# Long-convolution taps moved into the head stage, and output rows finished by ScalarE and accumulating transfers

## The chip, the cores and the metric

The kernel runs on one core of one Trainium2 chip. Its engines are TensorE (PE in the profile, with PEld for its weight loads), VectorE (DVE), ScalarE (ACT), GpSimd (POOL) and SyncE (SP, which issues most transfers). The metric is the device time of one execution in microseconds (us); a kernel's time is the median of its runs. SBUF is the on-chip memory that all engines read and write, PSUM the smaller one that TensorE writes its products into.

## The reference

One layer of a hybrid encoder on 512 rows of 2048 float32 values:

```python
h = rmsnorm(x, g_pre);  proj = h @ w_in
qkv, z_a, b, a, glu_in, z_b, gate_logits = split(proj)
# branch a: 16 heads of gated DeltaNet (conv of 4, chunks of 64, a triangular solve per chunk)
q, k, v = heads(silu(causal_conv(qkv, w_conv_qkv)))
o = gated_delta_chunked(l2norm(q), l2norm(k), v, g_log, beta)
y_a = (rmsnorm(o, g_dn_out) * silu(z_a)) @ w_br_a
# branch b: gated linear unit, causal depthwise convolution of 31 taps, layer norm over channels
u = causal_depthwise_conv(glu(glu_in), w_dw) + b_dw
y_b = (silu(layernorm(u, ln_g, ln_b)) * silu(z_b)) @ w_br_b
mixed = (gate_a * y_a + gate_b * y_b) @ w_out
x = x + rmsnorm(mixed, g_post)
e = p @ w_ple_proj
out = x + rmsnorm(sigmoid(x @ w_ple_gate) * e, g_ple)
```

## The kernel before

**Data.** Activations lie with channels on the 128 partitions and the 512 rows along the free axis in the first stages: a *channel tile* is 128 channels x 512 rows, and there are 16 of them for a width of 2048. At the end, rows lie on partitions: four *row tiles* of 128 rows, each in four column parts of 512. A float32 product is made of three matmuls, from a high and a low half of each operand (L183, L185 and L187 in `gemm_cm`). The halves of a weight piece are made on the fly by `prep`: ScalarE casts the high half (L126), and `low_part[0]` subtracts it from the raw weights to give the low half (L127). `low_part[0]` is VectorE, and GpSimd for a while in stage 2.

**What sets the order.** Matmul jobs stand in a list and run one after the other. After each 512-wide matmul, `tick()` counts down the generators that `spawn` has started; a generator whose count is zero runs to its next `yield n`, which means n more matmuls. So other engines' work is placed among the matmuls by counting them, and each engine executes in the order that results. `pin` keeps an instruction at its place in the program; the others may be reordered a little.

**Stages.** Loading and normalising x (to about 55 us); the z gates by a Strassen-like scheme (to 550); the heads (550 to 1487); *stage 2* (to 1960): the remaining gated pairs, the long convolution, branch a, layer norm; then branch b, the output projection and the end.

**Heads.** Eight pairs of heads, numbered 0 to 7 here. For each, six matmul tiles (k, q, v of two heads) and two tiles out of the deque `rest` are run, then `group(g)` is spawned. In `rest` stand the silu-gate tiles (`zb_tile`) and then the gated linear unit's tiles (`glu_b`, then `glu_a`). `group` goes: W on VectorE from a product in PSUM (L866, L867); four copies Ud on ScalarE, VectorE, GpSimd, VectorE (L881); a transpose UT (L887); the *triangular loop*, 31 steps of a multiplication (L898, both inputs in SBUF) and a reduction (L899) on VectorE, each depending on the last; a transpose Vd (L906); copies VP on ScalarE (L912) and transposes Tc on VectorE (L913); then TensorE's small products py (L919) and pz (L922), which need Tc, and pd (L934); then `head_scan` for both heads (psA L757, psB L763, psS L769, the output's transpose po L797). `scanning[0]` holds the number of the last pair whose scan has begun. VectorE also evacuates and convolves the q, k, v tiles there (L710) and makes the low weight halves (L127). In the same stage `presums` sums weight blocks in DRAM by 192 transfers from GpSimd's queue (L1070, L1075).

**Long convolution.** A finished gated tile u (L1041) goes into `waiting`. `convs` takes channel tiles from there, one at a time, and applies 30 taps on VectorE (L1011), `pace(s)` matmuls apart; in stage 2 `near` first copies u into PSUM (`up`), in the heads u is read from SBUF (`sg`). `side_convs` does two channel tiles in stage 2, each tap as a ScalarE product (L1032, `pr`) and a GpSimd addition (L1033). Finished tiles are added up for layer norm (`filtered`, L975 and L977); the sums over channels are matmuls (sum_ps L1195, the variance L1210, rstd_ps L1222).

**The end.** The gate product of the last step (L1635 to L1637) with its weight pieces from `split_piece` (ScalarE cast L1616, VectorE low half L1617) runs through a plan; after each quarter `step()` issues up to three of the queued `chores`. `gate_steps` weighs the embedding (sigmoid L1943, product L1944, square L1946, gain L1949); `final_steps(tt)` finishes a row tile: `inv_rms` (L1574, L1575 on VectorE, the power L1577 on GpSimd) and four times L1965 on VectorE (scale and add x1) with a store L1966. Row tiles 0 and 1 are `LOW`; tiles 2 and 3 come last, and the last tile's product is finished in two halves (L2038).

## Time and profile before

| | us |
|---|---|
| median of 3 runs (2391.45, 2393.43, 2393.59) | 2393.43 |
| the profiled execution, its own time | 2393.88 |
| span of the profiled execution, first to last instruction | 2391.8 |
| TensorE busy in the span | 2366.5 |
| VectorE busy in the span | 1909.5 |
| ScalarE busy in the span | 1230.6 |
| GpSimd busy in the span | 548.8 |
| VectorE busy in the heads (937 us) / in stage 2 (473 us) | 690.8 / 426.1 |
| GpSimd busy in the heads / in stage 2 | 213.5 / 263.5 |

The mean granted TensorE clock was 0.997 of full speed. The profile lists, per engine, line and operation, the busy time, the mean time of one in ns, and what ended the idle time before. A row of the timeline gives the start, the time until the last of the "xN" instructions ended, the engine, the line, what is written and read, and in brackets the idle time before and what released it.

### The profile page before, as it was taken

What the parts mean: (1) busy time and instruction counts of PE and PEld (TensorE: products, weight loads), DVE (VectorE), ACT (ScalarE), POOL (GpSimd) and SP (SyncE); (2) the same over time, 40 slices, a digit from 0 to 9 for tenths busy, and PEclk for the clock granted to TensorE, in tenths of its full rate; (3) what the DMA queues carried; (4) which work ended last, traced back from release to release, by engine and by line L of the source; (5) the groups of instructions that cost most, each with busy time, mean ns of one, the idle gap of its engine ahead of it and who ended that gap; (6) DMA issues with size and microseconds to landing.
All of it is one profiled execution on the core that took longest, in us unless ns stands there. A gap on an engine that the chain in (4) does not pass through costs nothing.

```text
span 2391.8 us, 33735 instructions
## 1 busy us (share of the span) xinstructions
PE 2366.5 (99%) x11774; PEld 1949.1 (81%) x11774; DVE 1909.5 (80%) x3517; ACT 1230.6 (51%) x2405; POOL 548.8 (23%) x591
## 2 busy tenths in 40 slices
PE   9999999999999999999999999999999999999997
PEld 7888888887888888888888887888888888888885
DVE  8877888786777786767777777999998897887877
ACT  6455455555644545454544544554423665665654
POOL 1001100011122122231321230798861000000000
PEclk9999999999999999999999999999999999999998
DMA  7577766665476768687874883443353577766565
GB/s 277 163 192 209 203 202 198 202 182 186 149 223 174 205 200 252 175 227 196 220 237 146 211 247 106 149 150 106 115 167 119 185 251 239 257 221 223 194 226 167
DMA packets 152186, 463.57 MB, mean 194 GB/s; under 512 B 17744, under 2 KB 26192, under 8 KB 150480
## 3 DMA queue, kind: packets, MB, share of 16 engines
q1 hardware_dynamic: 122608, 336.10, 41.9%
q0 software_dynamic: 27104, 121.13, 21.6%
q10 hardware_dynamic: 2304, 4.20, 0.6%
q8 instruction: 92, 1.51, 0.3%
q14 instruction: 78, 0.64, 0.1%
HBM read 426.22 MB, written 132.12 MB: 233 GB/s over the span
## 4 chain that ended last, share of the span: by engine, by line
PE 89%; DVE 4%; issue 2%; DMA 2%; ACT 2%; POOL 0%; SPq 0%; DVEq 0%; POOLq 0%; ACTq 0%
PE g L185 13%; PE g L187 13%; PE g L183 13%; PE zp L473 6%; PE zp L472 6%; PE zp L471 6%; PE f L1637 4%; PE f L1635 4%; PE f L1636 4%; PE yp L1466 2%; PE yp L1462 2%; PE yp L1464 2%; PE yp L1141 2%; PE yp L1143 2%; PE yp L1139 2%
## 5 line engine op out<-in xcount | busy, mean ns | idle before, releaser
L185 PE MATMUL g<-hl,w 128*128 128x512 f32 x1536 | 610.4, 397 | 0.0
L187 PE MATMUL g<-hh,w 128*128 128x512 f32 x1536 | 608.4, 396 | 0.0
L183 PE MATMUL g<-hh,w 128*128 128x512 f32 x1536 | 608.1, 396 | 0.0
L126 ACT CAST w<-raw 128x512 fp32r<-128x512 f32 x564 | 346.0, 617 | 415.6 <-PE g L187 240.7
L127 DVE TENSOR_TENSOR w<-raw,w 128x512 fp32r<-128x512 f32 x450 | 309.6, 695 | 86.4 <-ACT w L126 83.9
L185 PEld LDWEIGHTS g<-hl,w 128*128 128x128 f32 x1536 | 289.0, 188 | 55.4 <-issue 1.4
L183 PEld LDWEIGHTS g<-hh,w 128*128 128x128 f32 x1536 | 289.2, 188 | 54.1
L187 PEld LDWEIGHTS g<-hh,w 128*128 128x128 f32 x1536 | 289.1, 188 | 53.9 <-POOL w L127 0.3
L1011 DVE SCALAR_TENSOR_TENSOR uc<-up,vec,uc 128x497 f32<-128x497 f32 (+29 forms) x390 | 282.3, 733 | 13.2 <-ACT uc L990 1.9
L127 POOL TENSOR_TENSOR w<-raw,w 128x512 fp32r<-128x512 f32 x114 | 146.4, 1298 | 57.2 <-ACT w L126 55.1
L1635 PE MATMUL f<-wsp,oph 128*128 128x512 f32 x352 | 137.8, 391 | 0.0
L710 DVE SCALAR_TENSOR_TENSOR cv<-g,vec,cv 128x511 f32<-128x511 f32 x144 | 106.4, 739 | 39.2 <-ACT cv L708 38.9
L1636 PE MATMUL f<-wsp,opl 128*128 128x512 f32 x352 | 137.4, 390 | 0.0
L1637 PE MATMUL f<-wsp,oph 128*128 128x512 f32 x352 | 137.2, 390 | 0.0
L1617 DVE TENSOR_TENSOR wsp<-raw,wsp 128x1024 fp32r<-128x1024 f32 x81 | 98.5, 1221 | 31.0 <-ACT wsp L1616 25.5
L1616 ACT CAST wsp<-raw 128x1024 fp32r<-128x1024 f32 x81 | 83.8, 1048 | 63.1 <-PE f L1636 38.2
L1141 PE MATMUL yp<-w,oh 128*128 128x512 f32 x256 | 100.1, 391 | 0.0
L1143 PE MATMUL yp<-w,ol 128*128 128x512 f32 x256 | 99.5, 391 | 0.0
L1139 PE MATMUL yp<-w,oh 128*128 128x512 f32 x256 | 99.1, 389 | 0.0
L898 DVE TENSOR_TENSOR prod<-UT,VT 128x2 f32<-128x2 f32 (+30 forms) x248 | 87.2, 352 | 6.5
L1033 POOL TENSOR_TENSOR uc<-uc,pr 128x511 f32<-128x511 f32 (+29 forms) x60 | 75.7, 1262 | 8.3 <-ACT pr L1032 7.7
L1637 PEld LDWEIGHTS f<-wsp,oph 128*128 128x128 f32 x352 | 66.1, 188 | 13.9
(435 smaller groups left out, 4878.7 us busy)
## 6 DMA issues: line engine op xcount, KB each, us to landing
raw<-in_w_in SPq DMA_DIRECT2D x194, 512.0 KB, 3.7
wb_sums<-in_w_br_b POOLq DMA_DIRECT2D x48, 512.0 KB, 8.9
wo_sums<-in_w_out POOLq DMA_DIRECT2D x48, 512.0 KB, 8.9
wp_sums<-in_w_ple_gate POOLq DMA_DIRECT2D x48, 512.0 KB, 9.2
raw<-in_w_br_a SPq DMA_DIRECT2D x32, 512.0 KB, 3.3
raw<-wb_sums SPq DMA_DIRECT2D x32, 512.0 KB, 4.3
raw<-wp_sums SPq DMA_DIRECT2D x32, 512.0 KB, 3.7
raw<-in_w_ga SPq DMA_DIRECT2D x24, 512.0 KB, 5.1
```

The source lines that it names most:

```text
L126: nc.scalar.copy(hi, rq)
L127: low_part[0].tensor_tensor(lo, rq, hi.bitcast(F32), ALU.subtract)
L183: mm(ps, wh, rh, start=(k == 0), stop=False)
L185: mm(ps, wh, rl, start=False, stop=False)
L187: mm(ps, wl, rh, start=False, stop=(k == NK - 1))
L1011: pin(nc.vector.scalar_tensor_tensor(y[:, s:], u[:, 0:T - s], vv(w0 + TAPS - 1 - s), y[:, s:], ALU.mult, ALU.add))
L1139: mm(ps[tt], lh[:, b], wh, start=k == 0, stop=False)
L1141: mm(ps[tt], lh[:, b], wl, start=False, stop=False)
L1143: mm(ps[tt], ll[:, b], wh, start=False, stop=k == NK - 1)
L1635: mm(ps, lh, wh[:, c], start=kk == 0, stop=False)
L1636: mm(ps, ll, wh[:, c], start=False, stop=False)
L1637: mm(ps, lh, wl[:, c], start=False, stop=kk == 7)
```

## The change

Five things are edited.

1. `rest` holds the tiles of gated pairs 0 to 3 first, then the silu-gate tiles, then pair 4. The same 21 tiles run, seven of them after the last pair of heads.
2. `side_heads` is new, spawned with pair 1 of the heads: two channel tiles, each tap a ScalarE product (`pr`), 10 matmuls later a GpSimd addition, and 14 matmuls later the next one. `side_convs` with its two tiles in stage 2 stays.
3. `convs` is spawned with pair 3 and begins when pair 3's scan has begun, not pair 7's. While heads 3 to 6 are scanned, its taps are 18 matmuls apart. Two channel tiles are done in the heads; ten are left for VectorE's taps afterwards.
4. `with_x` stores x1 of row tiles 0 and 1 to `out` by eight transfers from GpSimd's queue, and the final steps of these tiles are a ScalarE scaling in place and a GpSimd transfer that accumulates into `out`. They are issued from a queue of their own, `scalings`, two per step.
5. The final steps of row tile 2 are woven between those of tile 3, after all matmuls.

TensorE executes the same instructions; psA, psB and psS of pair 3's scan stand up to six matmuls later, the last pair's po up to seven earlier, and the layer norm's sums 214 earlier.

```diff
--- before.py
+++ after.py
@@ -991,11 +991,11 @@
         return i, u, y
 
     def pace(s):
-        return (3 + s % 2 if taken_ps[0] else 4) if ups else CP
+        return (3 + s % 2 if taken_ps[0] else 4) if ups else CP if scanning[0] == NH // 2 - 1 else 18
 
     def convs():
         ready = last = None
-        while scanning[0] < NH // 2 - 1:
+        while scanning[0] < 3:
             yield 4
         while len(done) < NK:
             ready = ready or near()
@@ -1021,6 +1021,21 @@
                 taken_ps[0] = True
                 low_part[0] = nc.gpsimd
 
+    def side_heads():
+        for _ in range(SIDE):
+            while not waiting:
+                yield 4
+            i, u, y = near(False)
+            w0 = V_DW + i * TAPS
+            for s in range(1, TAPS):
+                pr = slots.tile([P, T], F32, tag="s", name="pr")
+                nc.scalar.activation(pr[:, s:], u[:, 0:T - s], AF.Copy, scale=vv(w0 + TAPS - 1 - s))
+                yield 10
+                pin(nc.gpsimd.tensor_tensor(y[:, s:], y[:, s:], pr[:, s:], ALU.add))
+                yield 14
+            nc.sync.dma_start(u_dram[i], y)
+            filtered(i, y)
+
     def side_convs():
         for _ in range(SIDE):
             while not waiting or not taken_ps[0]:
@@ -1079,7 +1094,8 @@
             for jp in range(2):
                 yield from f(jp, *args)
 
-    rest = deque([lambda i=i: zb_tile(i) for i in range(FILL, NK)] + [f for i in range(2) for f in (lambda i=i: glu_b(i), lambda i=i: glu_a(i))])
+    both = [f for i in range(5) for f in (lambda i=i: glu_b(i), lambda i=i: glu_a(i))]
+    rest = deque(both[:8] + [lambda i=i: zb_tile(i) for i in range(FILL, NK)] + both[8:])
     for g in range(NH // 2):
         pair = (2 * g, 2 * g + 1)
         for h in pair:
@@ -1089,6 +1105,10 @@
         jobs.append(lambda g=g: spawn(group(g), HP, "heads"))
         if g == 0:
             jobs.append(lambda: spawn(presums(), 16, "presum"))
+        if g == 1:
+            jobs.append(lambda: spawn(side_heads(), 8, "convs"))
+        if g == 3:
+            jobs.append(lambda: spawn(convs(), CP, "convs"))
         for _ in range(2):
             if rest:
                 rest.popleft()()
@@ -1096,9 +1116,8 @@
     mixed = [[None] * 4 for _ in range(NTT)]
     gate_b = [[None] * 4 for _ in range(NTT)]
 
-    jobs.append(lambda: spawn(convs(), CP, "convs"))
-    for i in range(2, 5):
-        glu_pair(i)
+    while rest:
+        rest.popleft()()
     run_jobs()
     finish("heads")
     heads_ctx.close()
@@ -1723,6 +1742,8 @@
         def with_x(j):
             for n, tt in enumerate(tts):
                 pin(nc.vector.scalar_tensor_tensor(x1[tt][j], x1[tt][j], rm[:, n:n + 1], xr.pop((tt, j)), ALU.mult, ALU.add))
+                if tt in LOW:
+                    nc.gpsimd.dma_start(rows(out, tt, j), x1[tt][j])
 
         def turn(k2, ps):
             for n in range(4):
@@ -1898,12 +1919,17 @@
 
     passed = [0]
 
+    scalings = deque()
+
     def step():
         next(xgen, None)
         passed[0] += 1
         for _ in range(2 if passed[0] < 20 else 3):
             if chores:
                 chores.popleft()()
+        for _ in range(2):
+            if scalings:
+                scalings.popleft()()
 
     pair = [-1]
 
@@ -1962,8 +1988,12 @@
 
         def one(j):
             e = e_t[tt, j]
+            if tt in LOW:
+                pin(nc.scalar.activation(e, e, AF.Copy, scale=rp))
+                pin(nc.gpsimd.dma_start(rows(out, tt, j), e, accum_op=ALU.add))
+                return
             pin(nc.vector.scalar_tensor_tensor(e, e, rp, x1[tt][j], ALU.mult, ALU.add))
-            nc.sync.dma_start(out[tt * P:(tt + 1) * P, j * T:(j + 1) * T], e)
+            nc.sync.dma_start(rows(out, tt, j), e)
         return [lambda j=j: one(j) for j in range(4)]
 
     v = {}
@@ -1999,7 +2029,7 @@
                 chores.append(chore_tt(d[t], ps[t], d[t], ALU.add))
             gated_out(LOW, 2 * jp + 1, d)
             if jp:
-                chores.append(lambda: chores.extendleft(reversed(final_steps(0) + final_steps(1))))
+                chores.append(lambda: scalings.extend(final_steps(0) + final_steps(1)))
         elif pr == "P7":
             u, s5 = v["P1", jp], v["Q5", jp]
             for t in range(2):
@@ -2020,28 +2050,28 @@
         for q in range(4):
             mms(ps[t], "Q4", last[q], q, t, x1_opnd)
             step()
-        while chores and t:
-            chores.popleft()()
         if t == 0:
-            late = deque([chore_tt(u[0], ps[0], u[0], ALU.add), *gate_steps(2, 2, u[0]), lambda: late.extendleft(reversed(final_steps(2)))])
-
-            def follow():
-                while late:
-                    late.popleft()()
-                    chores.append(follow)
-                    return
-            chores.append(follow)
-        else:
-            halves_ = [gate_steps(3, 2, u[1], h) for h in range(2)]
-            for h in range(2):
-                cs = slice(h * 256, h * 256 + 256)
-                pin(nc.vector.tensor_tensor(u[1][:, cs], ps[1][:, cs], u[1][:, cs], ALU.add))
-            for h in range(2):
-                halves_[h][0]()
-            for h in range(2):
-                halves_[h][1]()
-            for f in final_steps(3, 5):
-                f()
+            chores.append(chore_tt(u[0], ps[0], u[0], ALU.add))
+            chores.extend(gate_steps(2, 2, u[0]))
+    while chores:
+        chores.popleft()()
+    while scalings:
+        scalings.popleft()()
+    halves_ = [gate_steps(3, 2, u[1], h) for h in range(2)]
+    third = final_steps(2)
+    for h in range(2):
+        cs = slice(h * 256, h * 256 + 256)
+        pin(nc.vector.tensor_tensor(u[1][:, cs], ps[1][:, cs], u[1][:, cs], ALU.add))
+    third[0]()
+    for h in range(2):
+        halves_[h][0]()
+        third[1 + h]()
+    for h in range(2):
+        halves_[h][1]()
+    fourth = final_steps(3, 5)
+    third[3]()
+    for f in fourth:
+        f()
 
 
 def _cm_tiles(w, cols):
```

The first place is VectorE in pair 5's triangular loop. Before (`UT`, `VT` and `prod` are the loop's tiles, `w` and `raw` a weight piece):

```order
L898 TENSOR_TENSOR prod<-UT,VT 128x4
L899 TENSOR_REDUCE VT<-prod 128x1
L898 TENSOR_TENSOR prod<-UT,VT 128x10
L127 TENSOR_TENSOR w<-raw,w 128x512
L899 TENSOR_REDUCE VT<-prod 128x2
L898 TENSOR_TENSOR prod<-UT,VT 128x12
L899 TENSOR_REDUCE VT<-prod 128x2
L898 TENSOR_TENSOR prod<-UT,VT 128x14
```

In the changed kernel (`sg` is u, `uc` the channel tile's running sum):

```order
L898 TENSOR_TENSOR prod<-UT,VT 128x4
L899 TENSOR_REDUCE VT<-prod 128x1
L898 TENSOR_TENSOR prod<-UT,VT 128x10
L127 TENSOR_TENSOR w<-raw,w 128x512
L899 TENSOR_REDUCE VT<-prod 128x2
L1011 SCALAR_TENSOR_TENSOR uc<-sg,vec,uc 128x509
L898 TENSOR_TENSOR prod<-UT,VT 128x12
L899 TENSOR_REDUCE VT<-prod 128x2
L898 TENSOR_TENSOR prod<-UT,VT 128x14
L899 TENSOR_REDUCE VT<-prod 128x2
```

A tap of the long convolution (L1011) now stands between two steps of the loop, and so on at about every fourth step. The shapes of the loop's steps are the same.

The second place is GpSimd in pair 2 of the heads, in the changed kernel; before, only the transfers and the copies stood there (`wb_sums` and `wo_sums` are the weight sums in DRAM, `kq` a copy for the heads):

```order
L1085 DMA wb_sums<-in_w_br_b 128x1024
L1034 TENSOR_TENSOR uc<-uc,pr 128x488
L1085 DMA wb_sums<-in_w_br_b 128x1024 x2
L1034 TENSOR_TENSOR uc<-uc,pr 128x487
L1085 DMA wb_sums<-in_w_br_b 128x1024
L1034 TENSOR_TENSOR uc<-uc,pr 128x486
L1085 DMA wb_sums<-in_w_br_b 128x1024 x2
L1034 TENSOR_TENSOR uc<-uc,pr 128x485
L1085 DMA wo_sums<-in_w_out 16x8192
L1034 TENSOR_TENSOR uc<-uc,pr 128x484
```

The side taps' additions (L1034, `uc` plus `pr`) stand one by one between the transfers of `presums` (L1085 here, L1070 before).

The third place is VectorE at the end of the program. Before, from the last product of row tile 2 on:

```order
L1949 TENSOR_TENSOR e<-e,grow 128x512
L1574 TENSOR_REDUCE totp_21951<-ssp 128x1
L1575 TENSOR_SCALAR totp_21951<-totp_21951 128x1
L1965 SCALAR_TENSOR_TENSOR e<-e,rmsp_21954,snap 128x512
L1965 SCALAR_TENSOR_TENSOR ew<-ew,rmsp_21954,snap 128x512
L1965 SCALAR_TENSOR_TENSOR e<-e,rmsp_21954,u_20161 128x512
L1965 SCALAR_TENSOR_TENSOR e<-e,rmsp_21954,snap 128x512
L2038 TENSOR_TENSOR snap<-f,snap 128x256 x2
L1944 TENSOR_TENSOR e<-snap,e 128x256 x2
L1949 TENSOR_TENSOR e<-e,grow 128x256 x2
L1574 TENSOR_REDUCE totp_21986<-ssp 128x1
L1575 TENSOR_SCALAR totp_21986<-totp_21986 128x1
```

In the changed kernel L1965 is L1995, L1944 is L1970, L1949 is L1975 and L2038 is L2064:

```order
L1975 TENSOR_TENSOR e<-e,grow 128x512
L1593 TENSOR_REDUCE totp_22085<-ssp 128x1
L1594 TENSOR_SCALAR totp_22085<-totp_22085 128x1
L2064 TENSOR_TENSOR snap<-f,snap 128x256 x2
L1995 SCALAR_TENSOR_TENSOR e<-e,rmsp_22088,snap 128x512
L1970 TENSOR_TENSOR e<-snap,e 128x256
L1995 SCALAR_TENSOR_TENSOR ew<-ew,rmsp_22088,snap 128x512
L1970 TENSOR_TENSOR e<-snap,e 128x256
L1995 SCALAR_TENSOR_TENSOR e<-e,rmsp_22088,u_20275 128x512
L1975 TENSOR_TENSOR e<-e,grow 128x256 x2
L1593 TENSOR_REDUCE totp_22106<-ssp 128x1
L1594 TENSOR_SCALAR totp_22106<-totp_22106 128x1
```

Tile 2's four final steps stood ahead of tile 3's half additions and stand between tile 3's steps now. Eight L1965 of row tiles 0 and 1, which stood further ahead, are gone from VectorE.

## The prediction

> **What bounds the kernel now.** I read the page's busy shares first, then TensorE's waits, then the stretches in which another engine is nearly as full, and last the end.
>
> ```profile
> span 2391.8 us, 33735 instructions
> PE 2366.5 (99%) x11774; PEld 1949.1 (81%) x11774; DVE 1909.5 (80%) x3517; ACT 1230.6 (51%) x2405; POOL 548.8 (23%) x591
> PE po L797 <- DVE O L793: 1.6, 2, 0.8
> PE rstd_ps L1222 <- DVE dg L1217: 0.8, 1, 0.8
> PE f L1637 <- DVE wsp L1617: 0.7, 1, 0.7
> PE sum_ps L1195 <- POOL acc L977: 0.4, 1, 0.4
> ```
>
> TensorE is busy 99% of the span and its longest waits are under a microsecond (columns: total, times, longest). The change keeps every matmul. So it can win only these waits and what lies behind the last matmul; it loses whatever new wait TensorE gets. The losing side is much the longer one.
>
> Where is the cover thin? In the heads, each pair of heads has a stretch from W (L866) through the triangular loop (L898/L899) to the Tc transposes (L913), on which py (L919) waits. For pair 5, first VectorE and then TensorE:
>
> ```profile
> 1181.07 0.43 DVE L866 SCALAR_TENSOR_TENSOR W<-pg,E 128x256 f32<-128x256 f32 x1 [0.55 <-PE pg L862]
> 1221.59 1.38 DVE L913 STREAM_TRANSPOSE Tc<-VP 32x256 f32<-32x256 f32 x3
> 1225.37 0.69 PE L919 MATMUL py<-Tc,W 32*32 32x32 f32 x32
> 1198.48 0.69 DVE L127 TENSOR_TENSOR w<-raw,w 128x512 fp32r<-128x512 f32 x1 [0.84 <-ACT w L126]
> 1181.00:1223.00 42.00, 38.78 (x95) 1.00 0.67 206
> 1073.60:1181.00 107.40, 80.62 (x194) 1.00 0.73 201
> ```
>
> Tc ends at 1222.97 and py starts at 1225.37: slack 2.4 us. VectorE is busy 38.78 of 42.00 us there, with one removable gap, 0.84. So a stretch hides about 3.25 us of added VectorE time; beyond that py is late, and with it everything on TensorE. Over a whole pair (107.4 us) VectorE is busy 80.62, so work outside the stretch has room. The end is the second place:
>
> ```profile
> 2374.02 0.39 PE L1637 MATMUL f<-wsp,oph 128*128 128x512 f32 x1
> 2361.66 0.75 DVE L1965 SCALAR_TENSOR_TENSOR ew<-ew,rmsp,c 128x512 f32<-128x512 f32 x1 [0.60 <-POOL rmsp L1577]
> 2368.58 0.75 DVE L1965 SCALAR_TENSOR_TENSOR ew<-ew,rmsp,d 128x512 f32<-128x512 f32 x1
> 2369.24 1.28 DVE L1953 TENSOR_TENSOR snap<-f,snap 128x512 f32<-128x512 f32 x2
> 2381.65 0.75 DVE L2038 TENSOR_TENSOR snap<-f,snap 128x256 f32<-128x256 f32 x2
> 2385.30 0.75 DVE L1965 SCALAR_TENSOR_TENSOR e<-e,rmsp,snap 128x512 f32<-128x512 f32 x1 [0.66 <-POOL rmsp L1577]
> 2387.29 0.75 DVE L1965 SCALAR_TENSOR_TENSOR e<-e,rmsp,snap 128x512 f32<-128x512 f32 x1
> 2387.40 1.00 SPq L1966 DMA_DIRECT2D out_dram<-e  x2
> ```
>
> The last matmul ends at 2374.4; the tail of 17.4 us is VectorE's: it still works off row tiles 0 and 1 when the last products arrive, then tile 2, then tile 3.
>
> **The change, part by part.**
>
> *The end: -4.5 us.* Eight L1965 (four per tile 0 and 1) leave VectorE for ScalarE and accumulating transfers; from 2361.66 and 2362.33 they start 0.66 to 0.67 apart: 8 x 0.66 = 5.3 us of VectorE's work. Not all shows: the second weight piece in the row now waits for ScalarE's casts behind four scalings, so the L1953 pair starts about 2.9 us earlier (2366.3). Tile 3's half additions (L2038) no longer stand behind tile 2's four L1965; by walking the new order with the old durations they start near 2375.4 instead of 2381.65. In exchange those four are woven between tile 3's steps and cost +1.7 there, so the last group starts near 2380.6 instead of 2385.30. I take -4.5, with bounds -2.5 (weights' casts later still) and -5.5 (all 5.3 shows); it is 0 if one of the eight accumulating transfers lands last.
>
> *Layer norm: -1.0.* Ten channels instead of fourteen are left for VectorE after the heads, so the sums come 214 matmuls earlier in TensorE's order, and between the variance and rstd_ps there are 12 matmuls instead of 7. Five matmuls of 0.227 us (the L183 rows below) cover the 0.8 us wait. Bounds -1.2 and 0.
>
> ```profile
> 1224.15 0.39 PE L183 MATMUL g<-hh,w 128*128 128x512 f32 x1
> 1224.83 0.39 PE L183 MATMUL g<-hh,w 128*128 128x512 f32 x1
> ```
>
> Three matmuls in 0.68 us.
>
> *Taps of VectorE in pairs 4 to 6: +4.5.* convs() now starts its taps (L1011) with pair 3's scan, one in 18 matmuls. What does an instruction cost inside the loop?
>
> ```profile
> 1189.60 0.17 DVE L898 TENSOR_TENSOR prod<-UT,VT 128x4 f32<-128x4 f32 x1
> 1189.79 0.16 DVE L899 TENSOR_REDUCE VT<-prod 128x1 f32<-128x4 f32 x1
> 1189.99 0.18 DVE L898 TENSOR_TENSOR prod<-UT,VT 128x10 f32<-128x10 f32 x1
> 1190.08 0.69 DVE L127 TENSOR_TENSOR w<-raw,w 128x512 fp32r<-128x512 f32 x1
> 1190.68 0.16 DVE L899 TENSOR_REDUCE VT<-prod 128x2 f32<-128x10 f32 x1
> L1011 DVE SCALAR_TENSOR_TENSOR uc<-up,vec,uc 128x511 f32<-128x511 f32 (+5 forms) x297 | 217.4, 734 | 11.7 <-ACT uc L990 1.9
> ```
>
> From an L898 to its L899 it is 0.19 us without an L127 between and 0.69 with one: it costs 0.50, since it fills part of a dependent wait. A tap lasts 0.734 against 0.69, so I take 0.55 in the loop and 0.66 outside it. By the new order of VectorE, pair 4's stretch gets 9 taps (7 in the loop): 3.9 + 1.3 = 5.2; pair 5's 9 (8 in the loop) and one more L127: 5.5; pair 6's 7 and one L127, less one L1041: 3.7. Less 3.25 each: 1.95 + 2.25 + 0.45 = 4.65, taken as 4.5. Bounds: 0 (the transposes and copies hide more than I see) and 9.9 (0.66 everywhere, the 0.84 gap not filled).
>
> *Side taps on GpSimd in pairs 1 to 4: +11.2.* Each of the 60 puts an activation on ScalarE (51% busy, hidden) and a two-input addition on GpSimd. That would be free but for this, from the last part of the heads:
>
> ```profile
> L1011 DVE SCALAR_TENSOR_TENSOR uc<-sg,vec,uc x6: 718/726/1803, 1499.5 to 1504.2; 128x487 f32<-128x487 f32 x1, 128x486 f32<-128x486 f32 x1, 128x485 f32<-128x485 f32 x1, 128x484 f32<-128x484 f32 x1
> 1501.51 1.41 POOL L127 TENSOR_TENSOR w<-raw,w 128x512 fp32r<-128x512 f32 x1 [12.25 <-ACT w L126]
> 1504.23 1.29 POOL L127 TENSOR_TENSOR w<-raw,w 128x512 fp32r<-128x512 f32 x1 [1.31 <-ACT w L126]
> L1033 POOL TENSOR_TENSOR uc<-uc,pr x60: 1223/1262/1300, 1510.7 to 1745.6; 128x511 f32<-128x511 f32 x2, 128x510 f32<-128x510 f32 x2, 128x509 f32<-128x509 f32 x2, 128x508 f32<-128x508 f32 x2
> L898 DVE TENSOR_TENSOR prod<-UT,VT 128x2 f32<-128x2 f32 (+30 forms) x31 | 10.9, 352 | 0.8
> L127 DVE TENSOR_TENSOR w<-raw,w 128x512 fp32r<-128x512 f32 x13 | 8.9, 687 | 0.8 <-ACT w L126 0.8
> ```
>
> VectorE's taps that read both inputs from SBUF take 0.726 us (middle number), but up to 1.803 where GpSimd's additions run: up to 1.08 lost to one. The 297 taps with the input in PSUM keep their mean of 0.734 while GpSimd works on side taps. In the stretch L898 and L127 have both inputs in SBUF, 10.9 + 8.9 of 42 us, so an addition of 1.26 us almost always meets one; where a one-input instruction runs first, part is covered. I take 0.65 as the mean loss, an estimate; bounds 0.3 and 1.08. The stretch has 180 matmuls, one side tap in 24: 7.5, so 4.9 us. Pairs 1 to 3 also get one GLU product (0.5): 0.5 + 4.9 - 3.25 = 2.1 each, 6.3; in pair 4, where the taps have used the cover, all 4.9. Bounds of this part: +2.2 and +23.7.
>
> The Trainium skill, "SBUF — State Buffer", section "Who interferes with whom", says that a VectorE instruction with two SBUF inputs contends with a GpSimd instruction that reads SBUF, and that the loser is fully blocked for the whole instruction. The rows agree as to which taps suffer (1.803 against 0.734). By the full 1.26 us the stretch would lose an estimated 9.4 us, and this part would come to about 29.
>
> *Scans and weights outside the stretches: +1.* In pair 4 VectorE's 80.6 us become about 80.6 + 21 x 0.62 + 16 x 0.65 = 104 of 107.4, so weights and scans may be late now and then; 0 to 3. *Row stores of x1 by GpSimd, eight transfers near 2200: 0*, beside loads that have room; 0 to 1.5.
>
> **Sum.** -4.5 - 1.0 + 4.5 + 11.2 + 1 + 0 = +11.2. The profiled execution of 2393.9 us (span 2391.8 and 2.1 around it) becomes 2405.1, the span 2403.0. The median of the runs shown is 2393.43, 0.5 lower: **2404.6 us**.
>
> **Rivals.**
> 1. *Everything fits (the other side).* If the stretches hide all that is added, for instance because GpSimd's additions fall behind its own transfers into idle time and the taps fill waits, only the end and layer norm count: -5.5, 2387.9. It decides as long as py's slack is not used up, that is, while a stretch grows by no more than 3.25 us. For it: scans, copies and transposes leave gaps. Against it: nine taps alone make 5.2.
> 2. *No loss to GpSimd, but taps count.* Side taps are free: -5.5 + 4.5 + 1 = 0, 2393.4. Against it: the 1.803.
> 3. *Full blocking.* Each side tap costs 1.08, and VectorE, full in pair 4, delays scans by 2: -5.5 + 4.5 + 23.7 + 2 = +24.7, 2418.1. For it: both overlapped taps lost nearly this much; against it: L899 and L710 run alongside.
> 4. *The end is not won*, since GpSimd issues eight accumulating transfers in a row: +15.7, 2409.1.
>
> **Chances.** Forecast 0.42, own range 2396 to 2413; rival 1 0.16, rival 2 0.20, rival 3 0.14, rival 4 0.08. A measurement here can tell about 0.2%, 4.8 us, from no change. Faster by more: most of rival 1 and a little of rival 2, 0.16. Within: most of rival 2, the low end of the forecast, the rest of rival 1, 0.28. Slower: 0.56. Range 2388 to 2416: it leaves out half of rival 1 and of rival 3.
>
> **What would show it.** Right: waits of py on Tc in pairs 1 to 6, longest in pair 4 (about 6.9 us), none in pairs 0 and 7; L127 and L898 with longer means in pairs 1 to 4 than in 5 to 7; no wait at rstd_ps; the last group of L1965 starting about 6.2 us after the last matmul ends, not 10.9. Wrong: py without waits (rival 1), waits in pairs 4 to 6 alone (rival 2), ScalarE waiting for GpSimd to free a product's buffer and the casts queued behind it, or an accumulating transfer as the last to land.

## The result, and the profile after

The changed kernel takes 2450.06 us (2448.39 to 2452.86); the kernel before, run beside it, 2393.51 us. The ratio is 1.0238, with a 95% interval of 1.0225 to 1.0251: 56.6 us slower. The prediction was 2404.6 us, in a range of 2388 to 2416. Its sign was right; its size was a fifth of what came.

From the page of the changed kernel's profile, the span, the busy shares and four groups of instructions (number, busy time, mean ns, idle time before):

```profile
span 2451.1 us, 33846 instructions
PE 2391.6 (98%) x11774; PEld 1958.2 (80%) x11774; DVE 1920.0 (78%) x3465; ACT 1274.8 (52%) x2473; POOL 620.1 (25%) x651
L127 DVE TENSOR_TENSOR w<-raw,w 128x512 fp32r<-128x512 f32 x466 | 332.1, 718 | 107.0 <-ACT w L126 102.1
L710 DVE SCALAR_TENSOR_TENSOR cv<-g,vec,cv 128x511 f32<-128x511 f32 x144 | 106.5, 740 | 36.1 <-ACT cv L708 35.7
L898 DVE TENSOR_TENSOR prod<-UT,VT 128x2 f32<-128x2 f32 (+30 forms) x248 | 114.2, 461 | 6.3
L1034 POOL TENSOR_TENSOR uc<-uc,pr 128x511 f32<-128x511 f32 (+29 forms) x60 | 87.1, 1451 | 18.0 <-ACT pr L1032 17.5
```

And five of TensorE's waits in it (total, times, longest):

```profile
PE py L919 <- DVE Tc L913: 13.6, 9, 5.3
PE g L187 <- DVE w L127: 9.2, 7, 2.2
PE po L797 <- DVE O L793: 7.7, 6, 2.6
PE sum_ps L1214 <- POOL acc L977: 1.7, 1, 1.7
PE tp L1751 <- DVE snap L1744: 1.2, 1, 1.2
```

Before, no wait was longer than 1.5 us and none stood at py. TensorE runs the same 11774 matmuls in both, but is busy 25.1 us longer, so waits alone don't make the sum. Of the waits for VectorE, those of L187 for the low weight halves (L127) are the second largest, 9.2 us: the prediction had late weights outside the stretches alone, at +1 together with the scans.

Both programs run the same 512-wide matmuls, so the start of the n-th one in one trace, less its start in the other, shows where the time goes. Gain of that lag in us, by pair of heads (cut at the kernel before's pair borders; "side", "taps" and "narrow" are experiments below):

| pair | 1 | 2 | 3 | 4 | 5 | 6 | 7 | rest of the heads |
|---|---|---|---|---|---|---|---|---|
| the change | 12.1 | 7.4 | 10.8 | 16.5 | 6.5 | 1.2 | 5.9 | -0.3 |
| side tiles, no early taps (2428.5) | 12.5 | 6.6 | 8.2 | 6.0 | 0.2 | 0.0 | -0.1 | -0.1 |
| early taps, no side tiles (2407.3) | 0.0 | 0.0 | 1.3 | 2.9 | 4.9 | 3.2 | 0.1 | 5.5 |
| change with narrow additions (2407.6) | 0.5 | 0.6 | 1.6 | 3.0 | 5.9 | 1.2 | 3.9 | -1.6 |

In the changed kernel 60 of the lost microseconds stand in the heads. Behind them it loses 1.5 us at layer norm's sums and 1.3 us where x1 is stored, and the tail shrinks by 1.8 us (last matmul's end to the span's end, 15.6 us instead of 17.4). Ahead of pair 1 this execution was 1.7 us ahead of the kernel before; with that the pieces come to about the 59.3 us between the two spans.

The place to look at is pair 4's triangular loop. GpSimd first (its transfer issues are left out), then some of VectorE's rows, in the changed kernel:

```profile
1137.86 1.00 POOL L721 COPY kq<-kc 128x512 f32<-128x512 f32 x1 [15.77 <-ACT kc L719]
1139.36 1.56 POOL L1034 TENSOR_TENSOR uc<-uc,pr 128x487 f32<-128x487 f32 x1
1141.10 1.81 POOL L1034 TENSOR_TENSOR uc<-uc,pr 128x486 f32<-128x486 f32 x1
1144.93 1.50 POOL L1034 TENSOR_TENSOR uc<-uc,pr 128x485 f32<-128x485 f32 x1
1147.57 1.49 POOL L1034 TENSOR_TENSOR uc<-uc,pr 128x484 f32<-128x484 f32 x1
```

```profile
1137.83 0.54 DVE L898 TENSOR_TENSOR prod<-UT,VT 128x189 f32<-128x189 f32 x1
1138.41 0.35 DVE L899 TENSOR_REDUCE VT<-prod 128x7 f32<-128x189 f32 x1
1138.67 0.72 DVE L1011 SCALAR_TENSOR_TENSOR uc<-sg,vec,uc 128x495 f32<-128x495 f32 x1
1139.32 2.00 DVE L898 TENSOR_TENSOR prod<-UT,VT 128x196 f32<-128x196 f32 x1
1141.24 2.24 DVE L127 TENSOR_TENSOR w<-raw,w 128x512 fp32r<-128x512 f32 x1
1144.75 2.23 DVE L1011 SCALAR_TENSOR_TENSOR uc<-sg,vec,uc 128x494 f32<-128x494 f32 x1
1147.42 2.20 DVE L127 TENSOR_TENSOR w<-raw,w 128x512 fp32r<-128x512 f32 x1
```

Four additions stood behind the copy L721 in GpSimd's queue, which waited 15.8 us for its input; then they came 1.7 to 3.8 us apart. Each met a VectorE instruction with two inputs in SBUF, and that lasted 2.0 to 2.24 us instead of 0.54 to 0.72: about 1.5 us lost to each, more than the 1.08 I had as the upper bound. Summed over the VectorE instructions that overlap the 60 additions, each counted once, the time beyond the shortest of the same form is 48 us, 0.80 for each addition. The stretches from W to the last Tc have 36 of the additions and 37.7 of these microseconds, 1.05 each; the other 24 have 10.2, 0.43 each.

### The profile page after: what moved, and what is told of

Its sections match the earlier page's. It is cut to its first block, busy times and chain, and to the rows that moved or that the text cites. A ratio compares the mean times of both kernels' runs of the same rounds, so it can differ in the third digit from the quotient of the medians.

```text
span 2451.1 us, 33846 instructions
## 1 busy us (share of the span) xinstructions
PE 2391.6 (98%) x11774; PEld 1958.2 (80%) x11774; DVE 1920.0 (78%) x3465; ACT 1274.8 (52%) x2473; POOL 620.1 (25%) x651
## 3 DMA queue, kind: packets, MB, share of 16 engines
q8 instruction: 92, 1.51, 0.2%
## 4 chain that ended last, share of the span: by engine, by line
PE 76%; DVE 14%; ACT 3%; DMA 3%; issue 3%; POOL 1%; SPq 0%; POOLq 0%; DVEq 0%; ACTq 0%
PE g L187 10%; PE g L185 9%; PE g L183 9%; PE zp L471 6%; PE zp L472 6%; PE zp L473 6%; PE f L1656 3%; PE f L1655 3%; PE f L1654 3%; DVE w L127 3%; DVE prod L898 3%; PE yp L1160 2%; PE yp L1162 2%; PE yp L1158 2%; PE yp L1485 2%
## 5 line engine op out<-in xcount | busy, mean ns | idle before, releaser
L187 PE MATMUL g<-hh,w 128*128 128x512 f32 x1536 | 614.0, 400 | 9.2 <-DVE w L127 9.2
L127 DVE TENSOR_TENSOR w<-raw,w 128x512 fp32r<-128x512 f32 x466 | 332.1, 718 | 107.0 <-ACT w L126 102.1
L187 PEld LDWEIGHTS g<-hh,w 128*128 128x128 f32 x1536 | 292.1, 190 | 67.5 <-DVE w L127 13.2
L1011 DVE SCALAR_TENSOR_TENSOR uc<-up,vec,uc 128x511 f32<-128x511 f32 (+7 forms) x300 | 218.0, 734 | 16.8 <-ACT uc L990 8.0
L127 POOL TENSOR_TENSOR w<-raw,w 128x512 fp32r<-128x512 f32 x98 | 126.2, 1298 | 55.5 <-ACT w L126 31.4
L710 DVE SCALAR_TENSOR_TENSOR cv<-g,vec,cv 128x511 f32<-128x511 f32 x144 | 106.5, 740 | 36.1 <-ACT cv L708 35.7
L898 DVE TENSOR_TENSOR prod<-UT,VT 128x2 f32<-128x2 f32 (+30 forms) x248 | 114.2, 461 | 6.3
L1034 POOL TENSOR_TENSOR uc<-uc,pr 128x511 f32<-128x511 f32 (+29 forms) x60 | 87.1, 1451 | 18.0 <-ACT pr L1032 17.5
L721 POOL COPY kq<-kc 128x512 f32<-128x512 f32 x16 | 12.5, 780 | 306.0 <-ACT kc L719 252.4
```

The costliest lines, as they stand in the source:

```text
L127: low_part[0].tensor_tensor(lo, rq, hi.bitcast(F32), ALU.subtract)
L187: mm(ps, wl, rh, start=False, stop=(k == NK - 1))
L898: pin(nc.vector.tensor_tensor(pv_, um, vm, ALU.mult))
L1011: pin(nc.vector.scalar_tensor_tensor(y[:, s:], u[:, 0:T - s], vv(w0 + TAPS - 1 - s), y[:, s:], ALU.mult, ALU.add))
```

## Experiments

Theory A: GpSimd's additions hold VectorE's instructions that have two inputs in SBUF. Theory B: VectorE's own early taps are too much. Theory C: it is the place of the added work in GpSimd's and ScalarE's queues.

### Parts alone: no side tiles, no early taps, the end alone, narrow additions

Without the side tiles:

```diff
-        if g == 1:
-            jobs.append(lambda: spawn(side_heads(), 8, "convs"))
```

> The changed kernel without its two channel tiles on ScalarE and GpSimd in the heads; the early taps of VectorE, the new order of the gated tiles and the new end stay. Theory A (GpSimd's additions hold VectorE's instructions with two SBUF inputs for their whole length, 51 us of such holds more than before in the heads): most of the 56 us goes, 2400 to 2412 us, and what stays is py's waits in pairs 4 to 6, about 4 us each. Theory B (VectorE's own taps in the loop are what is too much): 2430 us or more.

Measured: 2412.1 us, ratio 1.0075 (1.0060 to 1.0090), at the upper edge of what theory A expected. Without side tiles VectorE found more gated tiles to start on, so it has a third early channel tile; the run with exactly two is below.

Without early taps, `convs` spawned after the last pair as before:

```diff
-        while scanning[0] < 3:
+        while scanning[0] < NH // 2 - 1:
```

> The changed kernel with the taps of VectorE begun with the last pair's scan, as before; the side tiles on ScalarE and GpSimd, the new order of the gated tiles and the new end stay. Theory A: pairs 1 to 3, which had no tap of VectorE until pair 3's scan, lost about 25 us in the changed kernel, and pair 4 loses as much as one of them, so 2420 to 2432 us. Theory B: 2405 us or less.

Measured: 2428.45 us, ratio 1.0142 (1.0127 to 1.0157). As theory A has it. Pair 1's stretch, from W to the last Tc, in the kernel before and then here (time, VectorE busy):

```profile
751.50:793.30 41.80, 38.57 (x95) 1.00 0.65 201
```

```profile
750.40:803.30 52.90, 50.74 (x97) 0.98 0.79 214
```

Two more instructions of VectorE (the new order of the gated tiles), 10 side additions on GpSimd: VectorE is busy 12.2 us longer without one tap of its own. The clock column fell from 1.00 to 0.98, of which more at the end.

The new end alone, on the heads and stage 2 of before; of the change's diff these pieces and their like:

```diff
+                if tt in LOW:
+                    nc.gpsimd.dma_start(rows(out, tt, j), x1[tt][j])
...
+            if tt in LOW:
+                pin(nc.scalar.activation(e, e, AF.Copy, scale=rp))
+                pin(nc.gpsimd.dma_start(rows(out, tt, j), e, accum_op=ALU.add))
+                return
```

> The kernel before with the new end alone (row stores of x1 by GpSimd, ScalarE scalings, accumulating transfers, tile 2's last steps between tile 3's). From the changed kernel's trace: the tail is 15.6 us instead of 17.4, and 1.3 us are lost at the x1 stores, so -0.5 us against before, 2393. By the prediction's term it would be -4.5, 2389.

Measured: 2392.61 us, ratio 0.9996 (0.9986 to 1.0006): the -5.5 us of the prediction's end and layer norm are not there.

The changed kernel with additions of 8 columns:

```diff
-                pin(nc.gpsimd.tensor_tensor(y[:, s:], y[:, s:], pr[:, s:], ALU.add))
+                pin(nc.gpsimd.tensor_tensor(y[:, s:s + 8], y[:, s:s + 8], pr[:, s:s + 8], ALU.add))
```

> The changed kernel with each of GpSimd's 60 additions in the heads cut to 8 of its columns (the rest of the addition is left out, so two channel tiles are not filtered fully); the ScalarE products, all waits and the order of every queue stay. Theory A: as without the side tiles, within 5 us of that run. Theory C (the additions cost by their place in GpSimd's queue, ahead of the copies and powers of the heads, and by the ScalarE products ahead of the casts): 2435 us or more.

Measured: 2407.58 us, ratio 1.0060 (1.0045 to 1.0075). The kernel leaves out most of each addition, so two channel tiles are not filtered; all waits, all queues and all ScalarE products are in place, and 42.5 us are gone. The length of the additions costs 42.5 us, their place nothing that shows, and theory C falls in this form. A long addition could still cost by occupying GpSimd's queue and not by holding VectorE; the loop with one input in PSUM and the additions in pieces, below, part these two. Step by step the change is -0.9 us for the end, 15.0 for the taps with narrow additions and 42.5 for the additions' length. The order of the steps counts: in the table the heads lose 60.1 us with both, 33.3 with side tiles alone and 17.9 with early taps alone, so some 9 us arise only where both meet, most of them in pair 4 (16.5, against 6.0 and 2.9).

### Additions kept out of the stretch

```diff
+                while in_loop[0]:
+                    yield 2
                 pin(nc.gpsimd.tensor_tensor(y[:, s:], y[:, s:], pr[:, s:], ALU.add))
```

Here `in_loop` is set from W to the last Tc of a pair, in the order of the program. GpSimd's queue runs behind that order at times, so 15 of the 60 additions still ran inside a stretch, instead of 36.

> The changed kernel with GpSimd's side additions held back while a pair is between W and the last Tc transpose; all else stays. If the additions cost time only where VectorE has no room (that stretch), the 42 us by which the changed kernel stands above the run with narrow additions fall to under 10: 2408 to 2417 us. If VectorE's holds cost elsewhere too (scans, the weights' low halves), 2425 us or more.

Measured: 2452.11 us, ratio 1.0244 (1.0230 to 1.0258). Not one microsecond is won. Pairs 1 to 3 lose less (3.8, 4.6, 6.6 us), but the additions now last until pair 6 and hold other instructions, for instance the output products of a scan. VectorE, then GpSimd, in this kernel:

```profile
953.51 1.14 DVE L793 SCALAR_TENSOR_TENSOR O<-O,ors,za 128x128 f32<-128x128 f32 x4 [1.15 <-POOL ors L789]
956.45 2.72 DVE L793 SCALAR_TENSOR_TENSOR O<-O,ors,za 128x128 f32<-128x128 f32 x4 [1.13 <-POOL ors L789]
```

```profile
956.99 1.24 POOL L1039 TENSOR_TENSOR uc<-uc,pr 128x492 f32<-128x492 f32 x1
```

And TensorE's waits in its heads:

```profile
PE po L797 <- DVE O L793: 12.9, 13, 2.0
PE py L921 <- DVE Tc L914: 10.1, 7, 5.0
PE psA L757 <- DVE S L774: 5.8, 4, 1.7
```

The sum of the holds is that of the change, 48 us, but 34 of them now stand outside the stretches, where the change had 10. So VectorE's idle time outside the stretch, 65.6 us of which it is busy 41, is no cover. The waits at po and psA say why: VectorE and TensorE take turns in the scans, and what holds VectorE in its turn holds TensorE.

### What is held: a loop with one input in PSUM, and additions in pieces

The run without early taps, with the loop's VT in PSUM:

```diff
-        VT = hd.tile([P, 32, 8], F32, tag="VT", name="VT", bufs=1)
-        nc.gpsimd.tensor_copy(VT.rearrange("p j i -> p (j i)"), cc(C_VI, 256))
+        VT = vps.tile([P, 32, 8], F32, tag="VT", name="VT")
+        nc.scalar.copy(VT.rearrange("p j i -> p (j i)"), cc(C_VI, 256))
```

`vps` is a PSUM pool of one buffer; the scans' pool gives up one of its four for it.

> The run without early taps of VectorE but with side tiles (2428 us), with the triangular loop's VT in PSUM instead of SBUF, so that L898 has one input in SBUF; ScalarE instead of GpSimd sets VT up. Theory A: L898 is no longer held (in the changed kernel 27 of 66 us of slowed VectorE instructions), L127 and the output products still are: 2408 to 2418 us, and the means of L898 are those of the kernel before. If any VectorE instruction is held, 2425 or more.

Measured: 2409.30 us, ratio 1.0065 (1.0051 to 1.0079): 19.2 us less than with VT in SBUF. Its control, the kernel before with the same edit:

> The kernel before with VT in PSUM (and ScalarE setting it up), as a control for the last: within 3 us of the kernel before, 2391 to 2397.

Measured: 2395.07 us, ratio 1.0010 (1.0001 to 1.0020). The groups of L898 and L127 from 640 to 1545 us, in the kernel before; with side tiles and VT in SBUF; and with VT in PSUM (there L898 is L899):

```profile
L127 DVE TENSOR_TENSOR w<-raw,w 128x512 fp32r<-128x512 f32 x256 | 176.9, 694 | 52.4 <-ACT w L126 50.9
L898 DVE TENSOR_TENSOR prod<-UT,VT 128x2 f32<-128x2 f32 (+30 forms) x248 | 87.2, 352 | 6.5
```

```profile
L127 DVE TENSOR_TENSOR w<-raw,w 128x512 fp32r<-128x512 f32 x255 | 189.7, 748 | 45.0 <-ACT w L126 40.8 <-PE pd L934 2.4
L898 DVE TENSOR_TENSOR prod<-UT,VT 128x2 f32<-128x2 f32 (+30 forms) x248 | 115.0, 464 | 6.6
```

```profile
L127 DVE TENSOR_TENSOR w<-raw,w 128x512 fp32r<-128x512 f32 x256 | 196.8, 772 | 57.0 <-ACT w L126 54.9 <-issue 0.2
L899 DVE TENSOR_TENSOR prod<-UT,VT 128x2 f32<-128x2 f32 (+30 forms) x248 | 82.9, 334 | 6.3
```

With one input in PSUM the loop's multiplications are not held: 334 ns with side tiles, 333 in the control, which has none. L127, still with both inputs in SBUF, is held more than ever (772 against 695 in the control). L710, with one input in PSUM, had 740 ns in the change and 739 before, though only 10 of its 144 met an addition; these took 694 to 766 ns. So what decides is where the second input lies. This is the rule that the prediction cited from the Trainium skill ("SBUF — State Buffer", "Who interferes with whom"), and the traces agree on it.

The additions of the changed kernel in four pieces of 128 columns:

```diff
-                pin(nc.gpsimd.tensor_tensor(y[:, s:], y[:, s:], pr[:, s:], ALU.add))
+                for c0 in range(0, T, P):
+                    cs = slice(max(c0, s), c0 + P)
+                    pin(nc.gpsimd.tensor_tensor(y[:, cs], y[:, cs], pr[:, cs], ALU.add))
```

> The changed kernel with each of GpSimd's 60 side additions cut into four instructions of 128 columns; the same sums. If a held VectorE instruction waits for the whole GpSimd instruction that holds it, a hold falls from about 1.4 us (39 of the 60 additions held one, 54 us in all) to about 0.4 to 0.5 and VectorE gets in between the pieces: below 2435 us. If what counts is the columns that GpSimd reads, however cut, 2445 us or more.

Measured: 2427.86 us, ratio 1.0143 (1.0129 to 1.0156): 22 us less than in one piece, for the same sums. A hold lasts about as long as the GpSimd instruction that makes it, so short ones let VectorE in between: 80 VectorE instructions lose 0.44 us each here, where 40 lose 1.17 in the change (those that lose over 0.1), and L898's mean is 396 ns instead of 461. GpSimd is not less occupied (240 pieces of 0.83 us, against 60 additions of 1.45), so the occupation of its queue is not what these 22 us were. (The 54 us in the expectation are 48 when each VectorE instruction is counted once and set against the shortest of its own form.)

### VectorE's taps and the order

The new order of the gated tiles and the new end, with neither side tiles nor early taps:

```diff
-        if g == 1:
-            jobs.append(lambda: spawn(side_heads(), 8, "convs"))
-        if g == 3:
-            jobs.append(lambda: spawn(convs(), CP, "convs"))
...
+    jobs.append(lambda: spawn(convs(), CP, "convs"))
     while rest:
         rest.popleft()()
```

> Only the new order of the gated tiles and the new end: no side tiles in the heads and no early taps of VectorE. If the order alone is free, as the prediction has it (0.5 us for one product in pairs 1 to 3, hidden), 2392 to 2394 us. If it is the order that costs the 15 us which the run with narrow additions still lost, 2405 us or more.

Measured: 2394.60 us (2391.41 to 2396.09), ratio 1.0004 (0.9995 to 1.0013), 0.6 above what was expected: the order costs nothing that can be told. In the profiled execution of this run 4.1 us were lost where x1 is stored (a wait at tp), against 0.9 to 1.4 in the other runs with the full new end, so as a base for the next run it may be some 3 us too high. Early taps for exactly two channel tiles on top of it:

```diff
+            if len(taken) == 2 and not ready and scanning[0] < NH // 2 - 1:
+                yield 1
+                continue
             ready = ready or near()
```

> The order of the gated tiles, the new end and VectorE's early taps for exactly two channel tiles; no side tiles at all. By the waits of the run with narrow additions (scans 8.5 us, po about 5, py 4) the taps of VectorE alone cost 12 to 16 us: 2404 to 2408. By the prediction's term (4.5 + 1, and the end as measured, -0.9) 2398.

Measured: 2407.34 us, ratio 1.0058 (1.0043 to 1.0073). The same as with narrow additions (2407.58), so the 60 ScalarE products cost nothing that shows, and the taps cost 13 us over the run before and 15 over the end alone. The table above has 17.9 us from pair 3 to the end of the heads (the tail is 3.0 us shorter than in the kernel before). Of these 4.3 stand at py and pz in pairs 4 to 6, where the prediction had 4.65. The largest other piece is at the end of the heads. VectorE and GpSimd in this kernel:

```profile
1494.08 1.14 DVE L793 SCALAR_TENSOR_TENSOR O<-O,ors,za 128x128 f32<-128x128 f32 x4 [0.94 <-POOL ors L789]
1496.84 3.95 DVE L793 SCALAR_TENSOR_TENSOR O<-O,ors,za 128x128 f32<-128x128 f32 x4 [0.90 <-POOL ors L789]
```

```profile
1498.44 2.20 POOL L977 TENSOR_TENSOR acc<-acc,uc 128x512 f32<-128x512 f32 x1
```

An early channel tile is added up for layer norm by GpSimd (L977) just when the last pair's output products run; the second group of L793 takes 2.8 us more than the first. It has two inputs in SBUF, so I take it for the same hold, from an instruction that I had not counted. The last L793, beside L977, loses 1.8 us of this. The other 1.0 is lost by one that ended just as L977's record begins, beside transfer issues that lengthened none of its L793 in the kernel before; whether L977 made that part too is open.

Two more runs asked what the rest is. First the 60 taps cut to 8 columns:

```diff
+                n = T if ups or len(taken) > 2 else s + 8
-                pin(nc.vector.scalar_tensor_tensor(y[:, s:], u[:, 0:T - s], vv(w0 + TAPS - 1 - s), y[:, s:], ALU.mult, ALU.add))
+                pin(nc.vector.scalar_tensor_tensor(y[:, s:n], u[:, 0:n - s], vv(w0 + TAPS - 1 - s), y[:, s:n], ALU.mult, ALU.add))
```

> The run with two early channel tiles (2407.3 us) with each of their 60 taps cut to 8 columns (the rest is left out, so two channel tiles are not filtered); order and waits stay. If the taps' length on VectorE is what costs: within 3 us of the run with the new order and end alone (2394.6). If the order costs: 2403 or more.

Measured: 2398.03 us (2394.71 to 2403.93), ratio 1.0020 (1.0010 to 1.0029): 3.4 us above the order and end alone, just outside what was expected, and the 2.8 us at L793 are still in its trace. So 9.3 us are the taps' length. Then no tap during a scan:

```diff
+                while in_scan[0] and not ups and scanning[0] < NH // 2 - 1:
+                    yield 2
```

> The run with two early channel tiles (2407.3 us) with the taps held back from the start of a pair's scans to their end in pairs 3 to 6; the taps left over follow with the last pair. If taps cost by standing among the scans' dependent instructions: the 7 us at the scans and 2 us at po go, py's part stays or grows a little: 2397 to 2402. If VectorE is just too full in these pairs, wherever the taps stand: 2404 or more.

Measured: 2405.12 us, ratio 1.0050 (1.0035 to 1.0065). Taps out of the scans went into the stretches, where the loss at py and pz rose from 4.3 to 6.9 us. So it is their length, and not their place, that VectorE has no room for in these pairs. The 7 us that I had put at the scans were also too many: the comparison counts a scan's small matmul that moved across a neighbour as lost there, and as won one matmul on.

### The end

Only row tile 0 by ScalarE and accumulating transfers, on the kernel before:

```diff
-            if tt in LOW:
+            if tt == 0:
                 pin(nc.scalar.activation(e, e, AF.Copy, scale=rp))
```

The x1 stores are cut to tile 0 likewise, and tiles 0 and 1 take turns in `scalings`.

> The kernel before with the new end, but only row tile 0 by ScalarE and accumulating transfers; row tile 1 is finished by VectorE and SyncE, one step of each in turn. In the new end GpSimd's power for tile 2 ran about 2.5 us late, behind the eight accumulating transfers. If that is what kept the tail at 15.6 us, four transfers leave GpSimd free in time and the tail is about 13: 2389 to 2390.5. If VectorE's four steps more take it back, 2392 or more.

Measured: 2389.66 us, ratio 0.9985 (0.9976 to 0.9994): the fastest version, 3.6 us below the kernel before. GpSimd's queue at the end of the changed kernel, and VectorE's first step for tile 2 behind it:

```profile
2424.36 2.71 POOL L1993 DMA_DIRECT2D out_dram<-ew  x3
2429.54 0.87 POOL L1993 DMA_DIRECT2D out_dram<-ew  x1 [2.47 <-issue]
2438.30 0.87 POOL L1993 DMA_DIRECT2D out_dram<-ew  x1 [2.66 <-ACT snap L1969]
2438.86 0.89 POOL L1596 TENSOR_TENSOR rmsp<-totp,mhalf_c 128x1 f32<-128x1 f32 x1
```

```profile
2436.57 0.15 DVE L1594 TENSOR_SCALAR totp<-totp 128x1 f32<-128x1 f32 x1
2439.79 0.75 DVE L1995 SCALAR_TENSOR_TENSOR e<-e,rmsp,snap 128x512 f32<-128x512 f32 x1 [2.40 <-POOL rmsp L1596]
```

The sum for tile 2's power was there at 2436.7; the last of the eight transfers stood ahead of it in GpSimd's queue and was issued only at 2438.30, and the power came at 2439.75. GpSimd sat idle for 2.66 us before that transfer. Its scaling had ended at 2433.5, so what it waited for is open. With one tile, GpSimd's queue is free in time:

```profile
2370.34 0.86 POOL L1974 DMA_DIRECT2D out_dram<-ew  x1 [6.29 <-ACT ew L1973]
2374.22 0.56 POOL L1577 TENSOR_TENSOR rmsp<-totp,mhalf_c 128x1 f32<-128x1 f32 x1 [3.02 <-DVE totp L1575]
```

The weaving of tile 2's steps between tile 3's alone, as a diff against the end alone:

```diff
-                if tt in LOW:
-                    nc.gpsimd.dma_start(rows(out, tt, j), x1[tt][j])
...
-            if tt in LOW:
-                pin(nc.scalar.activation(e, e, AF.Copy, scale=rp))
-                pin(nc.gpsimd.dma_start(rows(out, tt, j), e, accum_op=ALU.add))
-                return
...
-                chores.append(lambda: scalings.extend(final_steps(0) + final_steps(1)))
+                chores.append(lambda: chores.extendleft(reversed(final_steps(0) + final_steps(1))))
```

> The kernel before with only the last part of the new end: tile 2's final steps between tile 3's halves, after all matmuls; the eight steps of row tiles 0 and 1 stay on VectorE, no transfers from GpSimd. Tile 3's half additions no longer wait for tile 2's power (0.66 us) and its four steps, but the steps come in between later: 0.7 to 2 us less than before, 2391.3 to 2392.5. If the gain of the run with one tile (2389.7) is all in the weaving, 2389.7.

Measured: 2392.03 us, ratio 0.9994 (0.9985 to 1.0003): it can't be told from no change. So the weaving alone is not shown to make the gain of the run with one tile; that run's tail is 13.7 us in the profile, this one's 16.0.

## Why the prediction was wrong

- **Side tiles on GpSimd: the step that failed, +11.2 forecast, 42.5 measured.** The mechanism was right: which instructions are held, and that it decides the sign. Three sizes were off.
  - The hold: in the stretches 1.05 us per addition instead of 0.65, and 8 to 10 additions a stretch instead of 7.5, because they queue (behind L721 in pair 4) and come in bursts. That makes 37.7 us of holds in four stretches instead of 19.6; pair 1's stretch grew by 11.1 us where 0.5 + 4.9 was forecast.
  - The cover: I gave the stretches of pairs 1 to 3 3.25 us each. In the run with side tiles and no early taps the stretches of pairs 1 to 4 grew by 11.1, 6.5, 6.8 and 7.5 us and TensorE lost 10.2, 3.5, 5.3 and 6.0 there (with the slow clock below), so 0.9 to 3.0 us were covered. The sum let TensorE wait at py alone; it also waits inside the stretch for held low weight halves (in pair 1 of that run 1.8 and 1.7 us).
  - The rest of the pair: its holds were costed at nothing because VectorE is busy there only 41 of 65.6 us. There were 10.2 us of them, and the run with paused additions showed that holds there are paid too.
- **The third rival** (full blocking, 2418) named the right cause and was given 0.14. Its price of 1.08 per addition was nearly what the stretches showed (1.05), but with nothing lost outside them and full cover it was still 32 us short. (By its own terms the upper bound of the part is 24.2, not 23.7.)
- **VectorE's taps: +4.5 and +1 forecast, 13 to 15 measured.** The step at py was right (4.65 forecast, 4.3 found; 0.5 us for each in the loop), the "+1" for everything outside was not: the 2.8 us at L793 in the last pair and the slow clock after waits (below).
- **The end: -4.5 forecast.** The tail fell by 1.8 and the end alone made no difference. The step that failed is the start of the last group, 9.1 us after the last matmul and not 6.2: I walked VectorE's order and left out that GpSimd's power for tile 2 stands behind eight transfers that GpSimd issues (2.4 us). Rival 4 named the queue, but as a reason to lose it all.
- **Layer norm: -1.0 forecast, +1.5 found.** The wait at rstd_ps went, as expected, but the sums now come before GpSimd has added up the last channel tile (sum_ps waits 1.7 us for L977). With two early channel tiles and none on the side it is -0.3.
- **x1 stores: 0 forecast, 1.3 us lost** at the transposes of x1 (tp), within the bounds given; the run with order and end alone had 4.1.
- **What was to show it.** Waits of py with the longest in pair 4: right (5.3 us there, 6.9 forecast), but in pairs 1 to 5, and at pz in pair 6. Longer means of L898 in pairs 1 to 4: right (693, 571, 578 and 435 ns, and 351 to 352 in pairs 5 to 7); of L127: right in pairs 1 to 4 (728 to 839), but pair 5 has 742 too. ScalarE waiting for GpSimd to free a product's buffer: once, 1.8 us.

## What to carry to other kernels

Work for GpSimd is not free because GpSimd is idle: look up which VectorE instructions read two SBUF inputs while it runs, and charge the full length of the GpSimd instruction wherever such an instruction's result is awaited (here 1.05 us for an addition of 1.26 where VectorE was full). A low busy share is no cover where an engine takes turns with another: its idle time there is the other engine's turn. And a wait on TensorE can cost more than its length, by the clock below, so a sum of waits is a lower bound.

## What the runs showed of the hardware that was not expected

**After waits TensorE's clock fell to half for 3.4 us or more.** Some of TensorE's rows in the changed kernel, after the wait of 2.15 us in pair 4:

```profile
1143.53 0.50 PE L187 MATMUL g<-hh,w 128*128 128x512 f32 x1 [2.15 <-DVE w L127]
1144.67 0.63 PE L183 MATMUL g<-hh,w 128*128 128x512 f32 x1
1145.09 0.63 PE L185 MATMUL g<-hl,w 128*128 128x512 f32 x1
```

And three stretches of five us around py's wait of 5.3 us (length, TensorE busy, granted clock):

```profile
1155.00:1160.00 5.00, 1.92 (x44) 0.50 1.06 256
1160.00:1165.00 5.00, 5.00 (x35) 0.51 1.00 351
1165.00:1170.00 5.00, 5.00 (x51) 1.00 0.45 162
```

The 512-wide matmuls start 0.42 us apart instead of 0.227, some eight of them, then the clock is full again. The records of the clock have stretches of 3.4, 6.8 and 10.2 us at half. The heads of the kernel before have none; the changed kernel has seven with 48 wide matmuls, 0.2 us lost at each, and the run with two early channel tiles three with 28 (5.6 us). Small matmuls in these stretches are slower too (pz in pair 4 takes 1.97 us, 1.15 in the kernel before), which no sum of the prediction contained. The Trainium skill ("TensorE: Matmul & The Clock Gate", "HAM oscillation — how this bites in real kernels") gives a rule of no idle gaps over about 3.4 us; here a wait of 2.15 us, and several of under one microsecond among small matmuls, were enough, so the measurement is stricter than the rule. Not every such wait did it: after one of 1.8 us among wide matmuls, in pair 1 of the run without early taps, the clock stayed full. That the gate is what slowed these matmuls is read from the clock column; no run took the gate away.

**VectorE seems to hold GpSimd too.** Two powers of GpSimd stand in a row near the end. In the changed kernel, a long VectorE subtraction with both inputs in SBUF began 0.1 us before the second power; in the run with the new end alone, it began just after the second power did. GpSimd and VectorE in the changed kernel, then GpSimd in the run with the new end alone:

```profile
2422.36 2.06 POOL L1596 TENSOR_TENSOR rmsp<-totp,mhalf_c 128x1 f32<-128x1 f32 x2 [136.30 <-DVE totp L1594]
2422.78 1.23 DVE L1636 TENSOR_TENSOR wsp<-raw,wsp 128x1024 fp32r<-128x1024 f32 x1 [0.43 <-ACT wsp L1635]
```

```profile
2361.29 1.08 POOL L1577 TENSOR_TENSOR rmsp<-totp,mhalf_c 128x1 f32<-128x1 f32 x2 [136.17 <-DVE totp L1575]
```

The second power ended 0.4 us after the subtraction in the one; in the other neither was lengthened. The run with order and end alone shows the first case again (a power of 1.51 us, ending 0.4 us after the subtraction). No run varied this alone, so that VectorE held the power is read from the records. In the heads the records do not settle who came first: 20 of the 37 VectorE instructions that lost over 0.3 us began before the addition that they overlap, by the recorded starts.
